# Two-operand steps on VectorE instead of GpSimd, and modulation emitted later, in a two-layer transformer

## The chip, the cores and the metric

One core of a Trainium2 chip. The time is device microseconds of one execution, as the median of several runs; a profiled execution is taken beside them. The engines are TensorE (PE in the profile, with PEld its weight loads), VectorE (DVE), ScalarE (ACT), GpSimd (POOL) and SyncE (SP), whose queue issues all DMAs.

## The reference, cut to what matters

Two layers over 1024 latent tokens and 256 context tokens, 1024 features, all in float32. Each has a mixer (attention) and a feed-forward part with a convolution along the tokens; after each part comes a layer norm of the residual, and both are modulated by vectors computed from a condition.

```python
def conv_ffn(h, w_gate, w_up, conv_w, conv_b, w_down):
    g = h @ w_gate
    gp = jnp.pad(g, ((0, 0), (1, 1), (0, 0)))
    g = gp[:, :-2] * conv_w[0] + gp[:, 1:-1] * conv_w[1] + gp[:, 2:] * conv_w[2] + conv_b
    return (jax.nn.silu(g) * (h @ w_up)) @ w_down

def modulation(cond, w_mod, b_mod):
    return jnp.split(jax.nn.silu(cond) @ w_mod + b_mod, 6, axis=-1)

for i in range(DEPTH):                     # DEPTH = 2
    sh1, sc1, gt1, sh2, sc2, gt2 = modulation(c, w_mod[i], b_mod[i])
    o = mixer(x * (1 + sc1) + sh1)
    x = layer_norm(ALPHA * x + gt1 * o, ln1_g[i], ln1_b[i])
    f = conv_ffn(x * (1 + sc2) + sh2, ...)  # D_FF = 2816 = 22 x 128
    x = layer_norm(ALPHA * x + gt2 * f, ln2_g[i], ln2_b[i])
# the context tokens take the same path in layer 0 with c_ctx
```

## The kernel before

Features lie on partitions and tokens on the free axis. Every float32 product is made of three fp32r matmuls: each operand is split into a high part (ScalarE, `hi`, L82) and a low part (source minus high part, `lo`, L85), and high x high, high x low and low x high are added in PSUM (`mm`, L88). `lo` runs on GpSimd unless an engine is named.

The latent tokens come in two tiles of 512 (t = 0, 1), the context is t = 2. The stages are: layer 0's projections and attentions, `mixer_out` (output product, norms), `conv_ffn(N, 0)`, layer 1's projections and attention, `mixer_end`, `conv_ffn(N, 1)`.

**The feed-forward part** (`FeedForward`) multiplies 2 x 2 blocks with seven products, P1 to P7, instead of eight. In the up half, each of the 22 blocks f of 128 hidden features takes seven steps, one for each P; a step is 12 matmuls of 128x512 (four k, three part products). The tokens' operands of P6, P7, P5, P4 and P3 need both token tiles, those of P1 and P2 only tile 0. So P1 and P2 of the first `EARLY` = 8 blocks are done first (16 steps, here the first phase), while the norm of tile 1 and its operands (`norm`, `norm_operands`, `pair`) are still computed; their results go to DRAM (`pre_d`) and are read back (`again`). Then follow the other five steps of these 8 blocks (early blocks) and all seven of the other 14 (later blocks): 154 steps in all. `prepare` makes a step's weight operand: a sum of weight blocks where the P needs one (`add`, L1254, on VectorE), then its high and low part (`split`). `advance` prepares up to `RING` = 6 steps ahead. `evacuate` adds PSUM results on VectorE (L1364, tiles u, g, v); after P3, `finish` makes the convolution (L1391, L1392, on VectorE), the SiLU (ScalarE) and the product with v (L1394, GpSimd), and stores the block in DRAM (`hid_d`). `down_sums` forms sums of `w_down` blocks for the down half and stores them (`sum_d`), one pair of blocks after each odd f.

In the down half 77 steps follow: for each P, 11 steps j of 12 matmuls into four PSUM banks, with weights from `w_down` or `sum_d` and the hidden blocks read back into SBUF (`leave`, `load_hidden`) as tokens' operands. `hidden_operand` forms sums of hidden blocks (L1254, L1316, L1318) into a tile `sum`; `evacuate` adds each P's banks to the residual (`more`, L1476) at the end of its 11 steps. The hidden blocks of the second half and the residual of tile 1 are loaded when the up half ends.

**Modulation of layer 1** (`mod_vectors`) is computed on VectorE inside layer 0's up half: 12 chunks of 512 columns, each 8 products of a 128x512 tile of `w_mod` with a scalar per partition (L174, L176; for the first four chunks with two conditions, so twice as many), then the sum over partitions by small matmuls with a vector of ones (L183). It is a generator with 4 yields to a chunk; from the first early block on, each step runs it to its next yield.

**The norms** are generators too, in a list `behind`. `tick`, called after every third matmul, runs the first of them to its next yield, so that their work lies between matmuls. `norm` sums the eight feature tiles (partly on GpSimd, L336), takes the mean by a matmul (L359), subtracts it, squares (ScalarE) and sums, takes the statistics by small matmuls (L376), spreads the factor over partitions by a matmul (L273), and scales; k = 2, 5, 7 of the subtractions and scalings are GpSimd's (L346), from a copy of the PSUM tile by ScalarE (L341), the others VectorE's (L348).

`context` computes layer 0's feed-forward part of the context tokens, with 66 weight tiles in a row, each split in two halves.

The order of each engine's instructions is set by a scheduler from the order of emission and from priorities: weight loads are placed ahead by `rush` (100 instructions in the feed-forward parts), the ticks of layer 1's feed-forward part by `chain` (80). The engines then run their instructions in that order. All DMAs are in SyncE's queue, in order.

## Time and profile before

| | us |
|---|---|
| median of 3 runs | 3734.98 (3730.98 to 3742.63) |
| profiled execution, time | 3729.65 |
| profiled execution, span | 3727.8 |
| TensorE busy | 3273.4 |
| VectorE busy | 2668.0 |
| GpSimd busy | 1802.2 |
| ScalarE busy | 1653.1 |

The profile is of one execution; times in it are from the span's start. The profiled execution's own time is 1.85 us more than its span. A row of a group names the line, the engine, the operation, the tiles written and read, their shape and the count, then busy time and the mean of one in ns, then the idle time of the engine just before them and what ended it. A row of a stage gives start and end, length, and for each engine busy time and, in brackets, its instructions; then the granted clock of TensorE (1.00 is full speed), the busy share of the 16 DMA engines and GB/s. A row of a wait gives who waited, for whom, the sum in us, the count and the longest. L88, L82, L85 and L1254 are helpers' lines, so the tile names tell which use is meant: `al<-raw,ah` is the low part of a weight operand, `sum<-affy,siluc,sum` a product of modulation. Line numbers are those of the kernel before.

### The profile page before, as it was taken

Reading aid. Unit: us, or ns where it says so; the run is one execution under the profiler, and the core shown is the slowest. Engines: PE = TensorE matmul, PEld = TensorE weight load, DVE = VectorE, ACT = ScalarE, POOL = GpSimd, SP = SyncE. Lnnn points to the kernel's source line nnn. Section 1 sums busy time; section 2 is a strip of 40 time slices with the busy share of each in tenths; the row PEclk is TensorE's granted clock in tenths of the full one; section 3 lists DMA queues with packets and bytes.
Section 4 is the critical chain, followed back from the end, with each engine's and each line's share of the span. In section 5 each row is a group of like instructions: output and inputs, shape, how many; then the busy total and the mean of one; then the engine's idle time right before and its main releaser. Section 6 shows DMA issues by size and latency. Waiting matters only on the chain. (4 is left out here: it accounts for less than half of the span.)

```text
span 3727.8 us, 49048 instructions
## 1 busy us (share of the span) xinstructions
PE 3273.4 (88%) x16844; PEld 2667.7 (72%) x16844; DVE 2668.0 (72%) x4124; ACT 1653.1 (44%) x3153; POOL 1802.2 (48%) x1316
## 2 busy tenths in 40 slices
PE   8989999997666899898699999999899888999895
PEld 4467788885554688676598887887787666777674
DVE  2148888846777777589698467778897577776695
ACT  3126788824311233343454345556675432333333
POOL 4254344317633466455765334434423666665445
PEclk9999999998777899999799999999999889999997
DMA  7675143134456534633355665557554354345422
GB/s 222 200 209 175 60 102 86 48 108 140 145 168 204 172 128 144 257 91 108 118 178 164 187 179 159 142 157 208 167 153 137 116 173 165 131 144 201 162 84 71
DMA packets 282249, 555.55 MB, mean 149 GB/s; under 512 B 24144, under 2 KB 110608, under 8 KB 279952
## 3 DMA queue, kind: packets, MB, share of 16 engines
q1 hardware_dynamic: 282000, 552.42, 47.2%
q8 instruction: 133, 2.18, 0.2%
q14 instruction: 116, 0.95, 0.1%
HBM read 410.97 MB, written 141.36 MB: 148 GB/s over the span
## 5 line engine op out<-in xcount | busy, mean ns | idle before, releaser
L85 POOL TENSOR_TENSOR al<-raw,ah 128x512 fp32r<-128x512 f32 x374 | 561.8, 1510 | 352.7 <-ACT ah L82 335.9
L82 ACT ACTIVATE ah<-raw 128x512 fp32r<-128x512 f32 x418 | 255.1, 624 | 349.2 <-PE f L88 143.6
L85 POOL TENSOR_TENSOR al<-sum,ah 128x512 fp32r<-128x512 f32 x176 | 261.3, 1500 | 270.7 <-ACT ah L82 265.8
L88 PE MATMUL s<-k,q 128*128 128x512 f32 (+2 forms) x1152 | 306.7, 388 | 14.5 <-ACT sxc L1858 6.6
L85 DVE TENSOR_TENSOR ptl<-tp,pth 128x512 fp32r<-128x512 f32 x412 | 279.6, 684 | 43.3 <-ACT pth L544 38.6
L544 ACT ACTIVATE pth<-tp 128x512 fp32r<-128x512 f32 x412 | 241.8, 594 | 109.8 <-PE tp L540 103.4
L82 ACT ACTIVATE ah<-sum 128x512 fp32r<-128x512 f32 x264 | 161.0, 622 | 290.2 <-PE f L88 201.7
L88 PE MATMUL f<-al,ah 128*128 128x512 f32 x616 | 255.2, 414 | 33.2 <-DVE al L85 33.1
L540 PE MATMUL tp<-ident,p 128*128 128x128 f32 x1648 | 257.4, 276 | 20.4 <-DVE ptl L85 10.2
L88 PE MATMUL f<-ah,ah 128*128 128x512 f32 x616 | 247.9, 410 | 25.1 <-ACT ah L82 24.8
L88 PE MATMUL f<-ah,al 128*128 128x512 f32 x616 | 250.4, 407 | 3.2 <-POOL al L85 3.2
L88 PE MATMUL o<-pth,v 128*128 128x256 f32 x976 | 232.9, 300 | 4.6 <-ACT pth L544 4.5
L540 PEld LDWEIGHTS tp<-ident,p 128*128 128x128 f32 x1648 | 198.0, 142 | 51.6 <-DVE ptl L85 10.1
L88 PEld LDWEIGHTS s<-k,q 128*128 128x128 f32 (+1 forms) x1152 | 189.3, 192 | 44.4 <-ACT p L1871 9.9
L88 PE MATMUL o<-ptl,v 128*128 128x256 f32 x656 | 186.0, 295 | 17.6 <-DVE ptl L85 16.7
L85 POOL TENSOR_TENSOR wl<-wraw,wh 128x1024 fp32r<-128x1024 f32 x36 | 91.1, 2530 | 205.6 <-ACT wh L82 203.7
L88 PEld LDWEIGHTS o<-pth,v 128*128 128x128 f32 x976 | 171.6, 192 | 24.1 <-ACT pth L544 7.9
L1868 DVE TENSOR_REDUCE stat<-s 128x1 f32<-128x1024 f32 x128 | 155.5, 1216 | 37.8 <-PE s L88 37.3
L1871 ACT ACTIVATE p<-s,stat 128x1024 f32<-128x1024 f32 x128 | 142.5, 1114 | 79.9 <-DVE stat L1869 64.7
L1048 POOL TENSOR_SCALAR p<-p,stat 128x1280 f32<-128x1280 f32 (+1 forms) x80 | 94.0, 1178 | 172.3 <-ACT pth L544 59.5
L88 PEld LDWEIGHTS f<-al,ah 128*128 128x128 f32 x616 | 120.8, 196 | 77.4 <-DVE al L85 52.2
L88 PE MATMUL f<-T,ah 128*128 128x512 f32 x528 | 170.1, 404 | 0.2 <-DVE u L1364 0.2
(453 smaller groups left out, 10072.9 us busy)
## 6 DMA issues: line engine op xcount, KB each, us to landing
raw<-w_gate SPq DMA_DIRECT2D x82, 512.0 KB, 3.8
raw<-w_up SPq DMA_DIRECT2D x66, 512.0 KB, 4.7
raw<-w_down SPq DMA_DIRECT2D x66, 512.0 KB, 3.7
wm<-w_mod SPq DMA_DIRECT2D x96, 256.0 KB, 4.2
affy<-w_mod SPq DMA_DIRECT2D x96, 256.0 KB, 3.0
sd<-affy SPq DMA_DIRECT2D x88, 256.0 KB, 5.9
hid<-acc SPq DMA_DIRECT2D x44, 512.0 KB, 2.6
raw<-sd SPq DMA_DIRECT2D x88, 256.0 KB, 2.6
```

The source lines that it names most:

```text
L82: return self.nc.scalar.activation(out, src, AF.Copy)
L85: (eng or self.nc.gpsimd).tensor_tensor(out, src, hi.bitcast(F32), op=ALU.subtract)
L88: self.nc.tensor.matmul(out, lhsT, rhs, start=start, stop=stop)
L540: nc.tensor.transpose(ps[:, n * P : (n + 1) * P], pt[:, kc : kc + P], N.ident[:, :])
L544: nc.scalar.activation(h[:, : n * P], ps[:, : n * P], AF.Copy)
L1048: nc.gpsimd.tensor_scalar(p, p, st[:, 5, b : b + 1], 1.0, op0=ALU.mult, op1=ALU.mult)
L1868: nc.vector.tensor_reduce(st[:, 2, b, m : m + 1], s[:, :], axis=AX.X, op=ALU.max)
L1871: nc.scalar.activation(p[:, :SEQ], s[:, :], AF.Exp, bias=mx, scale=scale, accum_out=sums[:, b, m, 0:1])
```

## The change

- Norms: all sums over feature tiles run on VectorE into one total; of the subtractions k = 2, 5 stay on GpSimd; all scalings run on VectorE from PSUM, without the copy; one pass of statistics matmuls instead of two. `lag` = 3 yields are added in three places ahead of the matmuls. In `norm_parts` and `pair` some affine steps move to ScalarE, and `pair`'s last two low parts to VectorE.
- Modulation: its tiles are loaded two ahead into the tag `opt` (2 buffers, before `affy` with 3); a chunk has 6 yields, one of them between its last product and its matmuls; 72 yields are spread evenly over the 130 steps of the rest of the up half.
- `EARLY` is 12 instead of 8: 24 steps in the first phase (P1 of two blocks, then P2 of both), 12 early and 10 later blocks.
- Low parts of weight operands: on VectorE in the first phase; then GpSimd keeps P2, P7, P4 in the up half, and P5, P6, P4 in the down half. In `context` VectorE takes the first half of each tile.
- `finish`: the product with the gate runs on VectorE and writes s instead of v; the store of block f-1 is issued after P7 of block f. The last block's store, its load and the load of the second residual are issued after the second step of the down half.
- `down_sums` runs after P6 of each f below 11.
- Down half: the order is P1, P2, P5, P6, P7, P4, P3, and the sums of hidden blocks are made in place. The evacuations' VectorE instructions are queued (`late`) and emitted one after each group of three matmuls.

```diff
         nc = self.nc
+        todo = [(k, 1024 * which + 512 * half) for which, half, _ in chunks for k in range(KT)]
+        ws = []
+        def fetch():
+            k, c0 = todo.pop(0)
+            ws.append(self.t(wpool, [P, 512], tag="opt", bufs=2))
+            self.load(ws[-1][:, :], self.ins["w_mod"][l, k * P : (k + 1) * P, c0 : c0 + 512])
+        fetch()
+        fetch()
+        yield
...
             acc = {c: self.t(wpool, [P, 512], tag=f"sum{c}", bufs=1) for c in cs}
-            c0 = 1024 * which + 512 * half
             for k in range(KT):
-                w = self.t(wpool, [P, 512], tag="affy", bufs=3)
-                self.load(w[:, :], self.ins["w_mod"][l, k * P : (k + 1) * P, c0 : c0 + 512])
+                w = ws.pop(0)
...
                         nc.vector.scalar_tensor_tensor(acc[c][:, :], w[:, :], s, acc[c][:, :], op0=ALU.mult, op1=ALU.add)
-                if k % 2 and k < KT - 1:
+                if todo:
+                    fetch()
+                if k % 2:
                     yield
+            yield
...
         x = [self.acc[t][:, k, c0 : c0 + w] for k in range(KT)]
-        gp = (2, 5, 7)
+        gp = (2, 5)
...
-        def total(g):
-            return self.t(tmp, [P, 512], tag=f"{sums}{int(g)}", bufs=1)[:, :w]
-        def add(acc, k, src):
-            g = k in (1, 2, 5)
-            eng = nc.gpsimd if g else nc.vector
-            if g not in acc:
-                acc[g] = src
-                return
-            new = total(g) if any(acc[g] is y for y in x) else acc[g]
-            eng.tensor_tensor(new, acc[g], src, op=ALU.add)
-            acc[g] = new
+        def total(i):
+            return self.t(tmp, [P, 512], tag=f"{sums}{i}", bufs=1)[:, :w]
...
         def each(k, ps, c, op):
-            if k in gp:
+            if c is not None and k in gp:
...
         yield
-        acc = {}
-        for k in range(KT):
-            if k == KT - 1:
-                nc.vector.tensor_tensor(acc[False], acc[False], acc[True], op=ALU.add)
-            add(acc, k, x[k])
+        acc = total(0)
+        for k in range(1, KT):
+            nc.vector.tensor_tensor(acc, x[0] if k == 1 else acc, x[k], op=ALU.add)
...
                 yield
+        for _ in range(self.lag):
+            yield
         mean = psum()
-        nc.tensor.matmul(mean[:, :w], self.mean[:, :], acc[False], start=True, stop=True)
+        nc.tensor.matmul(mean[:, :w], self.mean[:, :], acc, start=True, stop=True)
...
         c = copy(mean)
-        acc, sq = {}, {}
+        acc, sq = total(1), {}
...
             if 1 <= k <= KT:
-                sq[k - 1] = total(k == 2) if k < 3 else self.t(tmp, [P, 512], tag="affy", bufs=3)[:, :w]
+                sq[k - 1] = acc if k == 1 else self.t(tmp, [P, 512], tag="affy", bufs=3)[:, :w]
                 nc.scalar.activation(sq[k - 1], x[k - 1], AF.Square)
-            if k >= 2:
-                add(acc, k - 2, sq[k - 2])
+            if k >= 3:
+                nc.vector.tensor_tensor(acc, acc, sq[k - 2], op=ALU.add)
+            yield
+        for _ in range(self.lag):
...
         for b in range(nb):
-            for g in (True, False):
-                nc.tensor.matmul(st[:, b : b + 1], acc[g][:, b * P : (b + 1) * P], self.mean[:, 0:1],
-                                 start=g, stop=not g)
+            nc.tensor.matmul(st[:, b : b + 1], acc[:, b * P : (b + 1) * P], self.mean[:, 0:1], start=True, stop=True)
...
         r = self.rstd(tmp, st[:, :nb], nb, 1.0, eps)
-        yield
-        yield
+        for _ in range(2 + self.lag):
+            yield
...
         yield
-        c = copy(bc)
...
             if k < KT:
-                each(k, bc, c, ALU.mult)
+                each(k, bc, None, ALU.mult)
...
             self.lo(h[1][:, k, :], ys[k][:, :w], h[0][:, k, :], eng=nc.vector)
-            if keep and k % 2:
+            if keep and k % 4 != 3:
...
             self.hi(t4[0][:, k, :], b)
-            self.lo(t3[1][:, k, :], c, t3[0][:, k, :], pool)
-            self.lo(t4[1][:, k, :], b, t4[0][:, k, :], pool)
+            self.lo(t3[1][:, k, :], c, t3[0][:, k, :], vec)
+            self.lo(t4[1][:, k, :], b, t4[0][:, k, :], vec)
             nc.scalar.activation(xa, xa, AF.Identity, scale=v[:, 2, k : k + 1], bias=v[:, 3, k : k + 1])
-            pool.tensor_scalar(xb, xb, v[:, 2, k + 4 : k + 5], v[:, 3, k + 4 : k + 5], op0=ALU.mult, op1=ALU.add)
+            nc.scalar.activation(xb, xb, AF.Identity, scale=v[:, 2, k + 4 : k + 5], bias=v[:, 3, k + 4 : k + 5])
...
-    ORDER = ("P1", "P2", "P6", "P7", "P5", "P4", "P3")
-    EARLY = 8
+    UP = ("P1", "P2", "P6", "P7", "P5", "P4", "P3")
+    DOWN = ("P1", "P2", "P5", "P6", "P7", "P4", "P3")
+    EARLY = 12
...
         self.raws, self.sums, self.parts = {}, {}, {}
-        first = [(f, p) for f in range(self.EARLY) for p in self.ORDER[:2]]
-        early = [(f, p) for f in range(self.EARLY) for p in self.ORDER[2:]]
-        rest = [(f, p) for f in range(self.EARLY, NF) for p in self.ORDER]
-        down = [(p, j) for p in self.ORDER for j in range(NF // 2)]
+        first = [(f + i, p) for f in range(0, self.EARLY, 2) for p in ("P1", "P2") for i in range(2)]
+        early = [(f, p) for f in range(self.EARLY) for p in self.UP if p not in ("P1", "P2")]
+        rest = [(f, p) for f in range(self.EARLY, NF) for p in self.UP]
+        down = [(p, j) for p in self.DOWN for j in range(NF // 2)]
...
             p, j = self.steps[n]
-            a = self.split(self.raws.pop(n))
+            a = self.split(self.raws.pop(n), None if p in ("P5", "P6", "P4") else self.N.nc.vector)
...
             src = self.add(a12, s[2], ALU.subtract)
-        self.parts[n] = self.split(src)
+        self.parts[n] = self.split(src, None if p in ("P2", "P7", "P4") and n >= self.n_first else self.N.nc.vector)
...
             return self.add(b12, b11, ALU.subtract)
-        t = self.add(b22, b12, ALU.subtract)
+        put = self.N.nc.vector.tensor_tensor
+        if p == "P6":
+            put(b12, b22, b12, op=ALU.subtract)
+            put(b11, b12, b11, op=ALU.add)
+            return b11
         if p == "P7":
-            return t
-        nc = self.N.nc
-        nc.vector.tensor_tensor(t, t, b11, op=ALU.add)
-        if p == "P4":
-            nc.vector.tensor_tensor(t, b21, t, op=ALU.subtract)
-        return t
+            return b12
+        put(b21, b21, b11, op=ALU.subtract)
+        return b21
...
             nc.scalar.activation(s, s, AF.Silu)
-            nc.gpsimd.tensor_tensor(v, v, s, op=ALU.mult)
-            N.load(self.hid_d[f][:, :], v)
-        ready = None
+            nc.vector.tensor_tensor(s, v, s, op=ALU.mult)
+        def store(f):
+            N.load(self.hid_d[f][:, :], s)
+        span, gone = self.n_up - self.n_first, 0
...
             if n >= self.n_first:
-                next(mods, None)
-                if p == "P6" and f % 2:
-                    self.down_sums(f // 2)
-                if p == "P4" and f + 1 < self.EARLY:
-                    ready = f + 1
+                while gone < 72 * (n - self.n_first) // span:
+                    next(mods, None)
+                    gone += 1
+                if p == "P6" and f < NF // 2:
+                    self.down_sums(f)
+                if p == "P7" and f:
+                    store(f - 1)
                 if p == "P3":
-                    if ready == f + 1:
-                        again(ready)
+                    if f + 1 < self.EARLY:
+                        again(f + 1)
+                    if f == NF - 1:
+                        self.leave(p)
                     finish(f)
-            if f == NF - 1:
+            if f == NF - 1 and p != "P3":
                 self.leave(p)
+        self.last = lambda: (store(NF - 1), self.load_hidden(1, (NF // 2 - 1,)), self.load_residual(1))
...
             self.places += [N.t(N.pbig, [P, 4, SEQ], tag=x) for x in ("b1h", "b1l")]
-            self.load_hidden(1, range(4, h))
-            self.load_residual(1)
+            self.load_hidden(1, range(4, h - 1))
...
+        late = collections.deque()
...
             a = N.acc[t][:, m, :]
-            nc.vector.scalar_tensor_tensor(a, src, gt[:, m : m + 1], a, op0=ALU.mult, op1=ALU.add)
+            late.append(lambda: nc.vector.scalar_tensor_tensor(a, src, gt[:, m : m + 1], a, op0=ALU.mult, op1=ALU.add))
...
                 more(0, 0, d, y)
-            elif p == "P6":
-                nc.vector.tensor_tensor(y, ps, y, op=ALU.add)
-                more(1, 0, d, y)
-            elif p == "P7":
-                nc.vector.tensor_tensor(y, ps, y, op=ALU.add)
-                more(0, 1, d, y)
-                more(1, 1, d, y)
...
                 more(1, 0, d, ps)
+            elif p == "P6":
+                late.append(lambda: nc.vector.tensor_tensor(y, ps, y, op=ALU.add))
+                more(1, 0, d, y)
+            elif p == "P7":
+                late.append(lambda: nc.vector.tensor_tensor(y, ps, y, op=ALU.add))
+                more(0, 1, d, y)
+                more(1, 1, d, y)
...
-        last = NF // 2 - 1
+        final = NF // 2 - 1
...
             if j == 0:
-                banks = [N.t(N.qq, [P, 512], tag="f") for _ in range(4)]
+                bank = [N.t(N.qq, [P, 512], tag="f") for _ in range(4)]
...
                 c = slice(d * P, (d + 1) * P)
-                ps = banks[d][:, :]
+                ps = bank[d][:, :]
...
                 N.mm(ps, ah[:, c], bl[:, :], False, False)
-                N.mm(ps, al[:, c], bh[:, :], False, j == last)
+                N.mm(ps, al[:, c], bh[:, :], False, j == final)
+                if late:
+                    late.popleft()()
                 N.tick()
-                if j == last:
+                if j == final:
                     evacuate(p, d, ps)
-            if j == last and p in ("P4", "P3"):
+            if n == self.n_up + 1:
+                self.last()
+            if j == final and p in ("P4", "P3"):
+                while late:
+                    late.popleft()()
...
                 r = raws[i]
-                parts.append([self.split(r[:, 512 * x : 512 * x + 512], nc.vector if x and i % 3 else None) for x in range(2)])
+                parts.append([self.split(r[:, 512 * x : 512 * x + 512], None if x else nc.vector) for x in range(2)])
```

2 lines of the change are left out of this document (added).

## The prediction

> **What bounds the kernel now.** I read the page first (busy shares and the slices), then busy time by stage, then the waits and groups of the worst stage, then single rows. TensorE is busy for 88% of the span, but three slices in a row show a granted clock of 0.7:
>
> ```profile
> PE 3273.4 (88%) x16844; PEld 2667.7 (72%) x16844; DVE 2668.0 (72%) x4124; ACT 1653.1 (44%) x3153; POOL 1802.2 (48%) x1316
> ...
> PEclk9999999998777899999799999999999889999997
> ```
>
> The stages that the change touches, in the order of the rows below: layer 0's first phase, its early blocks, a steady stretch inside the later blocks, all later blocks, the turn from up to down, down, down's last phase; then layer 1's first phase, up, turn, down, last phase, and the tail.
>
> ```profile
> core 0: us, PE busy (x) PEld busy (x) DVE busy (x) ACT busy (x) POOL busy (x), PEclk, DMA share, GB/s
> 911.00:985.50 74.50, 56.17 (x212) 43.12 (x212) 45.32 (x52) 34.02 (x59) 60.51 (x43) 0.82 0.50 172
> 985.50:1245.60 260.10, 155.01 (x593) 125.04 (x593) 201.97 (x268) 49.65 (x66) 93.89 (x56) 0.75 0.59 187
> 1300.00:1500.00 200.00, 200.00 (x862) 162.36 (x861) 148.49 (x152) 69.79 (x104) 129.81 (x82) 1.00 0.39 130
> 1245.60:1523.30 277.70, 277.06 (x1193) 224.85 (x1194) 210.85 (x226) 91.76 (x135) 170.52 (x107) 0.99 0.42 138
> 1523.30:1577.00 53.70, 37.01 (x133) 26.84 (x132) 24.94 (x23) 16.74 (x28) 19.28 (x12) 0.87 0.94 360
> 1577.00:1744.00 167.00, 155.63 (x662) 124.00 (x662) 149.32 (x165) 64.21 (x112) 82.81 (x56) 0.99 0.34 104
> 1744.00:1801.70 57.70, 45.69 (x155) 33.60 (x154) 38.15 (x43) 26.65 (x45) 45.29 (x34) 0.79 0.23 66
> 2929.80:3013.00 83.20, 58.95 (x221) 45.10 (x221) 57.61 (x61) 37.19 (x65) 68.68 (x49) 0.82 0.47 149
> 3013.00:3419.20 406.20, 389.92 (x1647) 310.33 (x1648) 303.89 (x314) 130.43 (x195) 256.87 (x157) 0.99 0.44 145
> 3419.20:3471.80 52.60, 37.31 (x134) 26.25 (x133) 23.18 (x25) 16.60 (x28) 16.52 (x11) 0.90 1.00 385
> 3471.80:3646.00 174.20, 162.24 (x677) 129.02 (x678) 156.88 (x172) 66.86 (x116) 88.46 (x61) 0.97 0.29 87
> 3646.00:3689.10 43.10, 35.98 (x136) 27.01 (x134) 25.64 (x30) 16.43 (x29) 27.14 (x21) 0.88 0.22 76
> 3689.10:3727.80 38.70, 7.85 (x20) 4.57 (x20) 17.02 (x23) 8.72 (x14) 17.25 (x15) 0.55 0.15 54
> ```
>
> 862 matmuls in 200 us are 0.232 us each, so a step (12 matmuls) is 2.78 us. Layer 0's 40 early steps are worth 111 us and took 260.1. Layer 1, which has no modulation to compute, took 406.2 us for 138 steps worth 384. What held layer 0's early steps:
>
> ```profile
> PE f L183 <- DVE sum L176: 99.7, 9, 18.4
> DVE modv L187 <- PE f L183: 15.8, 9, 2.8
> DVE sum L1254 <- DMA raw<-w_up: 11.6, 3, 6.0
> SPq L75 <- DVE sum L176: 65.1, 59, 4.0
> ...
> 1131.90 1.86 PE L183 MATMUL f<-ones,sum 128*128 128x1 f32 x8 [11.21 <-DVE sum L176]
> ```
>
> TensorE stands before modulation's column sums (L183) until VectorE has run through the products (L176), nine times, up to 18.4 us: one yield in each step puts modulation's 48 yields into 48 steps. VectorE is the near-bound there (202 of 260 us), and GpSimd makes it slower:
>
> ```profile
> L1364 DVE TENSOR_TENSOR acc<-f,acc 128x512 f32<-128x512 f32 x72 | 48.0, 683 | 22.4 <-DMA hid<-acc 20.0 <-DVE acc L1364 1.0 <-PE f L88 0.5
> L1392 DVE SCALAR_TENSOR_TENSOR acc<-acc,vecs 128x1023 f32<-128x1023 f32 x10 | 22.0, 2198 | 0.4
> L1254 DVE TENSOR_TENSOR sum<-raw,sum 128x512 f32<-128x512 f32 x10 | 15.8, 1577 | 3.9 <-POOL al L85 3.9
> L1391 DVE SCALAR_TENSOR_TENSOR acc<-acc,vecs 128x1023 f32<-128x1023 f32 x10 | 12.8, 1285 | 13.7 <-ACT acc L1390 13.7
> L1254 DVE TENSOR_TENSOR affy<-affy,raw 128x512 f32<-128x512 f32 x5 | 12.3, 2463 | 0.0
> L1254 DVE TENSOR_TENSOR sum<-raw,raw 128x512 f32<-128x512 f32 x10 | 6.8, 678 | 0.0
> L85 POOL TENSOR_TENSOR al<-raw,ah 128x512 fp32r<-128x512 f32 x31 | 45.8, 1491 | 6.7 <-ACT ah L82 6.7
> ```
>
> (The steady stretch.) The same two-operand form takes 0.678 us or up to 2.463; with one operand in PSUM (L1364) it is always 0.683. Over the three slow groups shown, the excess is 15.8-6.8, 12.3-3.4 and 22.0-12.8, 27 us; with the smaller groups about 40 us for 82 GpSimd instructions: an estimate of 0.5 us of VectorE for each.
>
> Single costs, uncontended:
>
> ```profile
> 3714.77 3.08 DVE L348 TENSOR_TENSOR acc<-acc,f 128x512 f32<-128x512 f32 x5 [2.86 <-ACT bcs L341]
> 3714.81 3.72 POOL L346 TENSOR_TENSOR acc<-acc,bcs 128x512 f32<-128x512 f32 x3 [3.63 <-ACT bcs L341]
> 3718.51 3.02 POOL L1610 TENSOR_SCALAR acc<-acc,vecs 128x512 f32<-128x512 f32 x4
> 1010.05 2.72 DVE L176 SCALAR_TENSOR_TENSOR sum<-affy,siluc,sum 128x512 f32<-128x512 f32 x4
> L85 DVE TENSOR_TENSOR wl<-wraw,wh 128x1024 fp32r<-128x1024 f32 x44 | 55.8, 1269 | 27.9 <-ACT wh L82 27.4
> ```
>
> In a row, VectorE does a 512-wide two-operand step each 3.08/5 = 0.62 us (GpSimd 1.24), a product 0.68, a 1024-wide step 1.27.
>
> **The change, part by part.**
>
> *Up, layer 0 (the largest term).* After the first phase 130 steps remain (12 blocks of 5, 10 of 7), 361 us of TensorE and some 17 us of column sums (an estimate: 16 groups, each 1.86 us at most by the row above, which ran at a low clock, so near 1 us). VectorE now has, in the 12 early blocks: evacuations 72, weight sums 48, down-sums 44 (now one block each, f<11), low parts 36 (P6, P5, P3): 200 x 0.62 = 124 us. Each block's end is two 1023-wide steps and the product that was GpSimd's, 2 x 1.28 + 1.27 = 3.8, x12 = 46. Modulation's 72 yields now lie over 130 steps, 33 of them here, with some 76 products: 52 us. Together 222 us against 167 of TensorE: VectorE becomes the bound of this stretch, and the covers it gave for nothing are gone. To it come 24 GpSimd low parts x 0.5 = 12, and waits. The waits (weights landing, modv: 27.4 us by the rows above) I bound by zero and by twice those rows, 55; I take about 25, since as many turns of the four weight buffers wait as before. In them lies SP's queue: modulation's loads now go through two buffers instead of three, each waits there for the product that frees one, as it did before (65.1 us), and pre's loads, hid's and the sums' stores stand behind; the weight loads are issued ahead of it. Early: 259 us. The 10 later blocks: VectorE 150 x 0.62 + 38 + 35 + 15 = 181, under TensorE's 195 + 7 = 202. Together 461. Before, the same 130 steps cost 537.8 (260.1 + 277.7) less 8 steps, 22.2, which now belong to the first phase: 515.6. **-54 us.**
>
> *Up, layer 1.* The same without products: early 124 + 46 + 12 + about 17 of waits = 199 against TensorE's 167; later 195. 394 against 406.2 - 22.2 = 384: **+10 us.** Here the change costs: the down-sums crowd into the 12 short blocks. What it gives back: hid's store no longer holds v (20.0 us of VectorE's idle in the steady stretch, hidden there by six prepared steps), so it counts nothing.
>
> *First phase.* 24 steps, 66.7 us, and 8 of norm matmuls. VectorE: norm 29, operand pairs 40, low parts 24, evacuations 12: 105 x 0.62 = 65, and 11 GpSimd steps x 0.5 = 6. In before the pairs pass between GpSimd and VectorE and TensorE runs dry after 16 steps; now it has 8 more. I take 82 (75 and 7 of stalls) in layer 0, 87 in layer 1, against 74.5 + 22.2 and 83.2 + 22.2: **-15, -18.** The longer norms (39 yields for 30, by the lag) no longer fit the 64 ticks of the pass before, so some of norm 2 is drained in front of the first phase: **+3** (between 0 and 8).
>
> *The turn from up to down.* It moves 360 and 385 GB/s with a DMA share of 0.94 and 1.00, so bytes are time here.
>
> ```profile
> raw<-w_down SPq DMA_DIRECT2D x66, 512.0 KB, 3.7
> sd<-affy SPq DMA_DIRECT2D x88, 256.0 KB, 5.9
> acc<-res SPq DMA_DIRECT2D x4, 2048.0 KB, 12.8
> ```
>
> The last down-sums (2 x 512 + 4 x 256 KB) are now eleven blocks earlier, and residual 1 (2048 KB) and the last hid load are issued two steps into down: 4.2 MB / 0.385 = 11 us, and SP's queue no longer holds weight loads behind the last store. I take **-10 each**; none if the hid loads alone fill the queues.
>
> *Down.* 662 and 677 matmuls (55 and 56 steps) are worth 154 and 157 us and took 167 and 174.2.
>
> ```profile
> PE f L88 <- DVE al L85: 15.2, 20, 2.2
> ```
>
> (Layer 1's down.) Sums in place cut P6, P7, P4 from 2, 1, 3 instructions to 2, 0, 1; with both low parts VectorE has at most 3 steps, 1.9 us, in a step of 2.78, and evacuations are spread one per slice. **-13 each.** In the last phase VectorE has 55 steps, 34 us (norm, 22 low parts, late sums), against 39 of TensorE: layer 0 from 57.7 to 44, **-13**; layer 1, **-5**.
>
> *Rest.* Tail: one matmul pass fewer and no ACT copy before the scaling, GpSimd's 3.72 off the end, against 3 more VectorE sums of 0.62: **-4**. The last mixer's norms **-3**. Context: a low part moves to VectorE in each triple (+), the norm at its start stalls less (-): 0. ACT's extra affine steps lie under its 56% of idle.
>
> Sum: 3 - 15 - 18 - 54 + 10 - 20 - 26 - 18 - 3 - 4 = -145. The profiled execution ran 3729.65 us (span 3727.8), so 3584.7; the median of the runs is 5.3 above it: **3590 us**.
>
> *A rule against the change.* Five steps in 3.08 us overlap their ends; alone one is 0.683. The Trainium skill ("VectorE: DVE Perf Modes", The DRAIN you can't avoid) says that the next operation does not start until the pipe is empty. By that rule the sum would be 3627 (the last of the rivals); by the row of five in 3.08 us it is 3590, and the rule does not hold here.
>
> **The rivals.**
>
> *VectorE keeps pace* (contention and waits vanish): early stretches 222 and 170 instead of 259 and 199: 3590 - 66 = 3524. For it: L1364's steady 0.683. Against: 24 low parts stay on GpSimd in each.
>
> *The stall stays* (the change doesn't do what it says): VectorE, in order, runs so late that TensorE still meets the column sums too early; layer 0's up stays at 515: 3644. For it: 222 us of VectorE in 167 us of steps. Against: sums are emitted two yields, about 3.6 steps, after their products.
>
> *VectorE binds both layers, and it gets slower.* If a two-operand step keeps costing what contention makes of it, up and the first phases run at VectorE's pace. With a cost r times 0.62, the early stretches grow by 392(r - 1) less the 24 counted for contention, layer 0's later blocks (166r) pass their 202 at r = 1.22, and each first phase (65r) its 85 at 1.31. At r = 1.36 (0.84 us a step) that is 117 + 24 + 7 = 148 and the gain is gone; at 1.45 it is 152 + 39 + 18 = 209, or 3799. For it: the steady stretch's sums cost 0.68 to 2.46. Against: GpSimd, 129.81 of 200 us there, falls to 24 steps in 259 us.
>
> *Operations do not overlap their ends*: the 610 two-operand steps of both early stretches (2 x 200) and first phases (2 x 105) at the single row's 0.683 instead of 0.62: 3590 + 37 = 3627. The five in 3.08 us speak against it.
>
> **How the numbers follow.** Forecast 0.62 (its own range 3545 to 3635), VectorE keeps pace 0.12, the stall stays 0.13, ends don't overlap 0.02, VectorE binds 0.11, of which a third ends within 0.3% of before, which is about what a measurement of this kernel can tell from no change. Faster 0.89, same 0.04, slower 0.07. The range goes from 3505 (VectorE keeps pace, turn and down at their best) to 3690 (the stall stays, and the wait bound of 55).
>
> **What would show it.** Right: no wait of L183 over 3 us; layer 0's up near 461 us, VectorE over 90% busy in its early blocks and its L1254 near 0.7 us; layer 1's early blocks slower than 2.78 us a step; no 13 us hole after the first phase; turns under 45 us. Wrong: L1254 still over 0.84 us, or TensorE still waiting for L176 by tens of us, or weight loads late behind SP's in-order waits.

## The result and the profile after

The changed kernel takes 3519.35 us in the median (3515.21 to 3524.63, four runs), the kernel before on the same chip 3738.81 (3730.98 to 3752.69): a ratio of **0.941, 95% interval 0.9378 to 0.9442**. The forecast was 3590. Its profiled execution took 3515.21 us (span 3513.4), against 3729.65 before: -214 where -145 was forecast. The line numbers have moved: high parts L82 are now L84, low parts L85 are L87, matmuls L88 are L90, products L176 are L187, column sums L183 are L197, weight sums L1254 are L1257, evacuations L1364 are L1369, and a block's end L1391, L1392, L1394 is L1396, L1397, L1399.

The page's busy times and granted clock:

```profile
PE 3205.5 (91%) x16772; PEld 2632.9 (75%) x16772; DVE 2650.5 (75%) x4518; ACT 1674.3 (48%) x3161; POOL 1097.7 (31%) x848
...
PEclk9999999999888899999899999999999999999998
```

GpSimd lost 705 us of work and VectorE has none the more in total, although it took most of these steps over. The stages, in order: layer 0's first phase, early blocks, later blocks, the hole at the turn (in which TensorE has next to nothing to do), the first part of down; the last mixer; layer 1's first phase, early blocks, later blocks, turn; and the tail.

```profile
core 0: us, PE busy (x) PEld busy (x) DVE busy (x) ACT busy (x) POOL busy (x), PEclk, DMA share, GB/s
904.80:992.60 87.80, 77.51 (x301) 60.38 (x302) 71.00 (x108) 47.32 (x82) 19.25 (x13) 0.88 0.61 203
992.60:1234.70 242.10, 198.69 (x793) 160.49 (x792) 226.75 (x325) 61.16 (x83) 37.94 (x24) 0.85 0.75 246
1234.70:1435.30 200.60, 200.60 (x889) 163.42 (x887) 174.66 (x253) 71.41 (x101) 36.67 (x28) 1.00 0.50 158
1435.30:1452.90 17.60, 1.81 (x9) 1.71 (x9) 7.16 (x8) 2.90 (x3) 0.00 (x0) 0.65 1.04 403
1452.90:1489.00 36.10, 36.10 (x150) 29.68 (x151) 20.94 (x34) 15.91 (x28) 0.00 (x0) 0.93 0.74 260
...
2728.00:2790.70 62.70, 56.86 (x232) 44.58 (x232) 44.70 (x63) 24.39 (x33) 19.37 (x14) 0.95 0.44 147
2790.70:2869.30 78.60, 72.36 (x301) 56.76 (x302) 70.74 (x107) 47.48 (x81) 19.48 (x13) 0.98 0.56 187
2869.30:3053.00 183.70, 174.05 (x721) 137.88 (x720) 172.17 (x223) 58.75 (x80) 46.33 (x23) 0.97 0.79 264
3053.00:3249.00 196.00, 196.00 (x841) 157.68 (x840) 146.08 (x193) 72.49 (x104) 40.03 (x29) 1.00 0.29 98
3249.00:3285.00 36.00, 32.72 (x135) 26.00 (x134) 22.39 (x33) 15.96 (x27) 0.00 (x0) 0.95 0.98 374
...
3480.20:3513.40 33.20, 6.00 (x13) 2.78 (x12) 19.60 (x32) 8.64 (x13) 6.61 (x7) 0.58 0.17 63
```

Both later stretches of up are full (TensorE 200.60 of 200.60 and 196 of 196). What is left lies in layer 0's early blocks (VectorE busy for 94%, TensorE 43 us short), the hole behind up, and the tail. Against the forecast's terms, with 22.2 us for the eight steps that moved into each first phase:

| part | forecast | measured |
|---|---|---|
| up to the first phase / context and odd attention / last mixer / tail | +3, 0, -3, -4 | -6.2, -14.2, -9.7, -5.5 |
| first phases, layers 0 and 1 | -15, -18 | -8.9, -26.9 |
| up after them, layers 0 and 1 | -54, +10 | -72.9, -4.2 |
| turn and down, layers 0 and 1 | -36, -28 | -27.2, -38.6 |
| sum | -145 | -214.3 |

The miss of 69 us is in two rows: 32 in the first (norms), 33 in the third (up). The second and the fourth row are near the forecast only as sums: in each, one layer gained 6 to 9 us less than forecast and the other 9 to 11 more. And the second and third row of layer 1 hang on a bound: the forecast ended the first phase of the kernel before at 3013.0, behind a hole; the table of stages below ends it at the next stage's first matmul, 2994.3. By that bound 18.7 us move from the one row to the other (-8.2 and -22.9 for -26.9 and -4.2).

What TensorE waited for most in layer 0's early blocks (the waits), and groups of VectorE there:

```profile
PE f L197 <- DVE sum L187: 39.1, 5, 12.2
```

```profile
L187 DVE SCALAR_TENSOR_TENSOR sum<-opt,siluc,sum 128x512 f32<-128x512 f32 x66 | 50.8, 812 | 2.3 <-DMA opt<-w_mod 2.2
...
L87 DVE TENSOR_TENSOR al<-sum,ah 128x512 fp32r<-128x512 f32 x35 | 28.7, 821 | 0.1
...
L1257 DVE TENSOR_TENSOR affy<-raw,affy 128x512 f32<-128x512 f32 x11 | 12.5, 1138 | 0.0
...
L1257 DVE TENSOR_TENSOR sum<-raw,sum 128x512 f32<-128x512 f32 x12 | 8.1, 678 | 0.0
```

The column-sum wait fell from 99.7 us to 39.1 but is there still. VectorE has next to no idle time, so the wait is no latency that a few yields could hide: VectorE is late because it is full. The same form costs 0.678 us or 1.138, as GpSimd works beside it or not; single rows of both are in the last section.

The hole at the turn, in order of time (timeline of VectorE, ScalarE and TensorE):

```profile
1443.40 1.24 ACT L1395 ACTIVATE acc<-acc,vecs 128x1024 f32<-128x1024 f32 x1 [7.51 <-DMA hid<-acc]
1444.68 1.28 DVE L1396 SCALAR_TENSOR_TENSOR acc<-acc,vecs 128x1023 f32<-128x1023 f32 x1 [7.28 <-ACT acc L1395]
...
1449.61 1.53 DVE L187 SCALAR_TENSOR_TENSOR sum<-opt,siluc,sum 128x512 f32<-128x512 f32 x2
...
1451.20 1.87 PE L197 MATMUL f<-ones,sum 128*128 128x1 f32 x8 [15.79 <-DVE sum L187]
```

The last products of modulation stand in VectorE's queue behind the last block's end, which stands behind the store of the block before. Spread over all 130 steps, modulation ends where nothing is left to hide it.

### The profile page after: what moved, and what is told of

Same layout as the page of the kernel before. It is cut to its first block, busy times and chain, and to the rows that moved or that the text cites. A ratio compares the mean times of both kernels' runs of the same rounds, so it can differ in the third digit from the quotient of the medians.

```text
span 3513.4 us, 48532 instructions
## 1 busy us (share of the span) xinstructions
PE 3205.5 (91%) x16772; PEld 2632.9 (75%) x16772; DVE 2650.5 (75%) x4518; ACT 1674.3 (48%) x3161; POOL 1097.7 (31%) x848
## 5 line engine op out<-in xcount | busy, mean ns | idle before, releaser
L87 POOL TENSOR_TENSOR al<-raw,ah 128x512 fp32r<-128x512 f32 x196 | 296.9, 1516 | 665.6 <-ACT ah L84 652.2
L84 ACT ACTIVATE ah<-raw 128x512 fp32r<-128x512 f32 x418 | 260.5, 630 | 434.3 <-PE f L90 294.8
L90 PE MATMUL s<-k,q 128*128 128x512 f32 (+2 forms) x1152 | 307.7, 389 | 15.8 <-ACT sxc L1877 6.8
L87 DVE TENSOR_TENSOR ptl<-tp,pth 128x512 fp32r<-128x512 f32 x412 | 279.6, 684 | 42.2 <-ACT pth L546 37.2
L84 ACT ACTIVATE ah<-sum 128x512 fp32r<-128x512 f32 x198 | 122.0, 629 | 342.9 <-DVE sum L1257 172.6
L542 PE MATMUL tp<-ident,p 128*128 128x128 f32 x1648 | 257.6, 276 | 20.7 <-DVE ptl L87 10.2
L90 PE MATMUL f<-al,ah 128*128 128x512 f32 x616 | 245.5, 398 | 10.5 <-DVE al L87 10.3
L90 PE MATMUL f<-ah,al 128*128 128x512 f32 x616 | 243.3, 395 | 7.5 <-POOL al L87 7.5
L90 PE MATMUL f<-ah,ah 128*128 128x512 f32 x616 | 241.3, 395 | 3.0 <-ACT ah L84 3.0
L90 PE MATMUL o<-pth,v 128*128 128x256 f32 x976 | 232.7, 300 | 4.6 <-ACT pth L546 4.5
L87 DVE TENSOR_TENSOR al<-raw,ah 128x512 fp32r<-128x512 f32 x222 | 173.7, 795 | 77.9 <-ACT ah L84 77.8
L90 PEld LDWEIGHTS s<-k,q 128*128 128x128 f32 (+1 forms) x1152 | 189.9, 193 | 45.7 <-ACT p L1890 10.8
L87 POOL TENSOR_TENSOR al<-sum,ah 128x512 fp32r<-128x512 f32 x44 | 67.8, 1541 | 426.0 <-ACT ah L84 384.3
L90 PE MATMUL o<-ptl,v 128*128 128x256 f32 x656 | 185.8, 295 | 16.3 <-DVE ptl L87 15.6
L90 PEld LDWEIGHTS o<-pth,v 128*128 128x128 f32 x976 | 171.2, 192 | 24.2 <-ACT pth L546 7.9
L1890 ACT ACTIVATE p<-s,stat 128x1024 f32<-128x1024 f32 x128 | 142.7, 1115 | 82.9 <-DVE stat L1888 67.6
L90 PE MATMUL f<-T,ah 128*128 128x512 f32 x528 | 168.7, 401 | 1.2 <-ACT ah L84 1.2
L90 PE MATMUL f<-b0h,ah 128*128 128x512 f32 x352 | 143.8, 409 | 14.4 <-ACT ah L84 8.8
L87 POOL TENSOR_TENSOR wl<-wraw,wh 128x1024 fp32r<-128x1024 f32 x36 | 91.2, 2533 | 202.7 <-ACT wh L84 200.8
```

The costliest lines, as they stand in the source:

```text
L84: return self.nc.scalar.activation(out, src, AF.Copy)
L87: (eng or self.nc.gpsimd).tensor_tensor(out, src, hi.bitcast(F32), op=ALU.subtract)
L90: self.nc.tensor.matmul(out, lhsT, rhs, start=start, stop=stop)
L542: nc.tensor.transpose(ps[:, n * P : (n + 1) * P], pt[:, kc : kc + P], N.ident[:, :])
L1890: nc.scalar.activation(p[:, :SEQ], s[:, :], AF.Exp, bias=mx, scale=scale, accum_out=sums[:, b, m, 0:1])
```

## The experiments

All are edits of the changed kernel; ratios are to the kernel before. Stage times of their profiles in us: the bounds are the first matmuls that read the next stage's operands; the hole at the turn is within "later 0"; kernels with 8 early blocks have 16 steps in the first phase and 40 in the early blocks, for 24 and 60.

| kernel | start | first 0 | early 0 | later 0 | down 0 | odd | mixer | first 1 | early 1 | later 1 | down 1 | tail | span |
|---|---|---|---|---|---|---|---|---|---|---|---|---|---|
| before (8 early) | 911.0 | 74.5 | 260.1 | 277.7 | 278.2 | 1052.9 | 75.4 | 64.5 | 139.0 | 285.9 | 269.8 | 38.7 | 3727.8 |
| changed | 904.8 | 87.8 | 242.1 | 218.2 | 233.4 | 1038.7 | 65.7 | 78.5 | 183.8 | 196.0 | 231.2 | 33.2 | 3513.4 |
| norms back | 914.6 | 90.3 | 237.1 | 218.1 | 241.6 | 1045.2 | 73.5 | 86.9 | 185.0 | 195.2 | 235.2 | 38.2 | 3561.0 |
| GpSimd back | 901.3 | 84.6 | 272.4 | 235.5 | 232.7 | 1039.8 | 66.4 | 78.8 | 203.6 | 200.2 | 231.8 | 33.2 | 3580.3 |
| eager modulation | 899.6 | 89.8 | 292.4 | 204.8 | 234.5 | 1042.0 | 65.5 | 78.5 | 184.8 | 196.0 | 233.3 | 33.2 | 3554.4 |
| pacing 22 + 50 | 903.0 | 86.7 | 210.6 | 226.0 | 234.1 | 1038.2 | 65.5 | 78.3 | 184.6 | 195.2 | 234.6 | 33.2 | 3490.0 |
| modulation on TensorE | 904.7 | 86.6 | 211.1 | 241.7 | 234.1 | 1041.9 | 65.9 | 78.2 | 188.7 | 195.2 | 231.7 | 33.2 | 3513.0 |
| turn back | 902.6 | 89.6 | 242.0 | 218.5 | 233.4 | 1042.7 | 67.1 | 79.9 | 184.9 | 195.2 | 230.4 | 33.2 | 3519.4 |
| down back | 903.5 | 89.8 | 242.9 | 218.3 | 244.9 | 1043.5 | 65.5 | 78.6 | 184.0 | 196.0 | 245.2 | 33.2 | 3545.3 |
| 8 early blocks | 903.3 | 64.8 | 163.1 | 308.1 | 232.8 | 1041.8 | 67.6 | 60.4 | 124.8 | 275.1 | 229.9 | 33.2 | 3505.0 |
| sums back | 903.2 | 86.6 | 220.0 | 235.2 | 233.2 | 1035.2 | 65.6 | 78.5 | 168.8 | 201.6 | 236.2 | 33.6 | 3497.6 |
| no GpSimd | 903.1 | 86.7 | 240.4 | 218.0 | 233.2 | 1042.0 | 65.5 | 78.6 | 185.1 | 195.2 | 233.6 | 33.6 | 3514.9 |
| split modulation | 904.7 | 88.1 | 199.3 | 206.1 | 233.9 | 1043.8 | 66.9 | 78.6 | 186.7 | 195.2 | 232.9 | 33.3 | 3469.5 |
| sums spread too | 900.0 | 89.8 | 198.9 | 219.9 | 234.2 | 1044.1 | 65.8 | 78.4 | 172.8 | 195.8 | 230.2 | 33.9 | 3463.7 |

Where an edit does not touch them, start lies between 899.6 and 904.8, odd between 1035 and 1044, and each of the other stages within 5 us.

**Norms back.** `norm`, `norm_parts` and `pair` as in the kernel before; a line of `pair`:

```
-            self.lo(t3[1][:, k, :], c, t3[0][:, k, :], vec)
+            self.lo(t3[1][:, k, :], c, t3[0][:, k, :], pool)
```

> The changed kernel (3515.21 us profiled), with the token norms and the last mixer's VectorE steps as in the kernel before: steps and sums shared with GpSimd, two chains of sums, a copy of the scaling factor, no extra yields ahead of TensorE's sums. Theory of the forecast: outside the first phases the norms are worth little (start +3, context 0, last mixer -3, tail -4, last phases some -5), so the time comes back by 9 us, and by some 6 in each first phase through GpSimd's contention: about 3535. Rival, from the changed kernel's stages (start -6, context -9.5, last mixer -9.7, tail -5.5, all without an edit other than the norms' in front of them): the norms alone hold 31 us there and 10 to 20 in the first phases: 3555 to 3570, with TensorE again 8 us late for the first sum at the context's start.

3563.49 us, ratio 0.9561 (0.9545 to 0.9578): the rival is right. The norms hold 48 us: start 9.8, odd 6.5 (no more than it varies by), mixer 7.8, tail 5.0, together 29; layer 1's first phase 8.4; the downs, with their last phases, 8.2 and 4.0. TensorE again waits 7.6 us for the first sum at the context's start. Where the time goes is seen in TensorE's waits in the last mixer, first with the norms back, then in the changed kernel:

```profile
PE f L90 <- ACT wh L84: 6.1, 1, 6.1
PE f L390 <- POOL sum L350: 3.0, 1, 3.0
PE f L90 <- DVE wl L87: 2.1, 1, 2.1
```

```profile
PE f L380 <- DVE sum L373: 4.6, 1, 4.6
PE f L90 <- ACT wh L84: 0.5, 1, 0.5
```

The wait for the norm's own sum is no shorter (4.6 for 3.0). What went is the wait for the next weights, 8.2 us, whose two parts stand behind the norm's steps in ScalarE's and VectorE's queues: with the norms back, the ScalarE step in front of `wh` itself waits 1.8 us for GpSimd.

**GpSimd back.** `self.parts[n] = self.split(src)` in up, and the block's last product on GpSimd.

> The changed kernel with all low parts of up's weight operands and each block's last product on GpSimd again; modulation, norms, down and the 12 early blocks stay changed. Theory A (VectorE's time bounds the early blocks, and each GpSimd instruction costs it 0.5 to 0.8 us): in layer 0's early blocks VectorE loses 36 low parts and 12 products (38 us) and gains 48 GpSimd instructions (24 to 38 us), so they stay within 15 us of 242; the first phases lose VectorE 24 low parts each. In all 3490 to 3530. Theory B (the move to VectorE carries up's gain): the early blocks of both layers and the first phases come back towards the time before, 3560 to 3600, with VectorE's sums at over 1.2 us and low parts late.

3584.40, ratio 0.962 (0.9602 to 0.9637): theory B's time, and its early blocks: layer 0's lose 30 us, layer 1's 20. Its first phases did not come: they are no longer than the changed kernel's (84.6 and 78.8 for 87.8 and 78.5). Window and groups of layer 0's early blocks, then what TensorE waited for there and in layer 1's:

```profile
985.90:1258.30 272.40, 198.43 (x794) 160.21 (x793) 238.16 (x288) 64.63 (x91) 128.67 (x75) 0.82 0.69 224
```

```profile
L187 DVE SCALAR_TENSOR_TENSOR sum<-opt,siluc,sum 128x512 f32<-128x512 f32 x64 | 68.6, 1115 | 0.7 <-DMA opt<-w_mod 0.7
...
L1257 DVE TENSOR_TENSOR sum<-raw,sum 128x512 f32<-128x512 f32 x13 | 13.1, 1011 | 1.9 <-POOL al L87 1.9
```

```profile
PE f L197 <- DVE sum L187: 69.6, 5, 20.9
```

```profile
PE f L90 <- POOL al L87: 19.9, 19, 2.4
```

In layer 0 VectorE does 37 instructions fewer (288 for 325) and is busy 11 us longer: a product costs 1.115 us for 0.812. Taking off the 36 low parts at 0.68 and 11 products of a block's end at 1.22 leaves 189 of 226.75; it was busy 238, 49 us more, of which some 5 are other steps that fell into the window: some 45 us for 51 more GpSimd instructions. In layer 1 (busy 168.82 for 172.17) the same sum gives 29 us for 48, where 36 were saved. **A step handed to GpSimd costs VectorE about as much as doing it.** The time goes two ways: in layer 0 the products come later, and the column sums' wait grows from 39.1 us to 69.6; in layer 1, which has no products, TensorE waits 19.9 us for GpSimd's own low parts (4.1 in the changed kernel).

**Eager modulation** (`next(mods, None)` once a step) and **pacing 22 + 50**:

```
-                while gone < 72 * (n - self.n_first) // span:
+                i, e = n - self.n_first, 5 * self.EARLY
+                while gone < (22 * i // e if i < e else 22 + 50 * (i - e) // 62):
```

> The changed kernel with one yield of modulation in each step again, so that its 72 lie in the first 72 of 130 steps. Theory A (VectorE's time is the bound in layer 0's early blocks): 27 more yields, some 42 products at 0.68 to 0.77 us, fall into them, and they grow from 242 by about 30; the later blocks stay at TensorE's pace, and the 15.8 us wait of the column sum at the turn goes: about 3530. Theory B (TensorE's waits there are the latency of each group of sums, not VectorE's load): the early blocks stay within 8 us of 242 plus the sums that moved in (5 groups of 1.9 us), and the turn gains 16: about 3505.

> The changed kernel with 22 of modulation's 72 yields in the 60 early steps (33 before) and the other 50 in the 62 steps after, none in the last 8. Theory A (VectorE bounds the early blocks, with 15 us of idle; the later blocks have 26 us of VectorE to spare): early 242 - 11 x 112/72 x 0.77 = 229, later unchanged at 200 to 203, the turn without its 15.8 us wait: about 3487. Theory B (waits are latency): early stays at 235 to 242, later grows by the sums, the turn still gains: about 3500. Theory C (the later blocks have no room left): later over 210, about 3500 with VectorE at over 95% there.

3556.24 (0.9545, 0.9527 to 0.9563) and 3493.44 (0.9375, 0.9358 to 0.9391). In the early blocks theory A in both, and more than it said: they go from 242 to 292 (30 more expected) and to 210.6 (229 expected). Early blocks of the eager one, its waits, and the paced one, with a wait of its later blocks:

```profile
989.30:1281.70 292.40, 209.72 (x825) 170.17 (x824) 251.65 (x375) 63.05 (x83) 35.84 (x24) 0.80 0.71 236
```

```profile
PE f L197 <- DVE sum L187: 82.7, 9, 14.4
DVE acc L1369 <- PE f L90: 20.8, 13, 3.6
```

```profile
989.60:1200.20 210.60, 188.01 (x769) 146.55 (x768) 200.46 (x281) 57.77 (x79) 38.74 (x23) 0.94 0.76 256
```

```profile
PE f L197 <- DVE sum L187: 13.8, 4, 10.2
```

A product costs more than its own 0.77 us. At a column sum TensorE, in order, stands still though operands are ready (ScalarE waits 87.4 us there for TensorE to free their buffers, for 36.3 in the changed kernel); then VectorE has no evacuations to do and idles in its turn (20.8 us for 2.8), so the two take turns. With fewer products TensorE meets the sums late enough, the wait for L187 falls to 0.9 us, and VectorE alone sets the pace (200.46 of 210.60). The later blocks took the rest (218.2 with the hole, 226.0 without): TensorE meets column sums too early there now, once by 10.2 us, so part of the gain is given back. This is theory C's sign (over 210), though VectorE is busy for 92% there, not 95%.

**Modulation on TensorE.** Products and column sums replaced by

```
+                    nc.tensor.matmul(ps[:, 128 * j : 128 * j + m], w[:, j * P : (j + 1) * P], self.siluc[:, k, :m],
+                                     start=k == 0 and j == 0, stop=k == KT - 1 and j == 3)
```

> The changed kernel with modulation's products left to TensorE: for each 128-row piece of the weights four matmuls with a 128x1 or 128x2 silu operand add up in one PSUM bank (384 small matmuls in place of 112 VectorE products and 16 groups of column sums); loads and pacing stay, through four buffers. Theory A (VectorE's time is what holds layer 0's up): 112 x 0.77 = 86 us leave VectorE, TensorE pays 384 x 0.12 = 46 less 15; layer 0's early blocks come to 190 to 200 (layer 1 takes 183.8 without products), all of its up, turn wait included, to 415 to 430 from 460.3: about 3475. Theory B (waiting at the modulation is latency of its loads, whoever computes): TensorE now waits for the weights' DMA instead and the early blocks stay above 225: 3500 or more.

3510.69 (0.9414, 0.94 to 0.9428), no faster than the changed kernel. The time is theory B's (3500 or more), but not by its cause: the early blocks come to 211, not over 225, and TensorE waits for the weights' DMA 3.2 us in all of up. Early and later blocks:

```profile
991.40:1202.50 211.10, 207.94 (x1058) 175.20 (x1057) 177.45 (x248) 61.37 (x83) 34.73 (x24) 0.98 0.82 275
1202.50:1444.10 241.60, 241.60 (x1257) 204.67 (x1256) 143.55 (x204) 72.62 (x101) 36.08 (x28) 1.00 0.43 141
```

VectorE is freed as theory A has it, but my price for TensorE was wrong. Its busy time in up is 449.5 for 361 of steps, so the 384 matmuls cost some 88 us, 0.23 each; each is recorded as two, and I had taken the record's 0.12 for the matmul.

**Turn back, down back.**

```
-        self.last = lambda: (store(NF - 1), self.load_hidden(1, (NF // 2 - 1,)), self.load_residual(1))
+        store(NF - 1); self.load_hidden(1, (NF // 2 - 1,)); self.load_residual(1)
```

and for the other `hidden_operand`, `run_down`, the order of the phases and the low parts' engine as before.

> The changed kernel with the last store of the hidden blocks, the last hidden load and the second residual's load issued at the end of up again, not two steps into down. Theory of the forecast (bytes bound the turn; each turn gained about 10 us through these later issues and the earlier sums together): down with its turn grows by some 5 us in each layer from 233.4 (layer 0) and 231.2 (layer 1), 3525. Rival (the hidden loads alone fill the queues; the turn's gain comes from the down-sums' earlier place): no stage moves by more than 2 us, 3515.

> The changed kernel with down's inner part as before: token sums in new tiles (2, 1 and 3 instructions for P6, P7, P4), weight operands' low parts all on GpSimd, evacuations at once after each phase, the order of the phases as in up; the late loads stay. Theory of the forecast: -13 in each layer's down and part of the last phase's -13 and -5 come back: down from 233.4 and 231.2 to about 250 each, 3548. Rival (down's gain came from the turn and from the norms in its last phase): under 5 us in each layer, 3520.

3521.22 and 3547.09 (one run each). The late issues are worth nothing (233.4 and 230.4 in the downs): the rival. Down's inner part is worth 11.5 and 14.0, with what it does in the last phase: near the forecast's 13 each, and under the 17 and 19 that were expected here with a part of the last phases' terms.

**8 early blocks** (`EARLY = 8`).

> The changed kernel with 8 early blocks in place of 12. Theory A (up is bound by VectorE, which has about 18 us of work a block in layer 0, against 13.9 us of TensorE's in an early block and 19.5 in a later one): four blocks that become later ones are no longer held, layer 0's first phase and up go from 548 to about 533, layer 1's from 458 to 450: about 3492. Theory B (the eight steps more of the first phase are what the norms of the second half are hidden behind): the first phases run dry again by 15 to 20 us each before the first P6, and the time is 3515 to 3545.

3509.22 (0.9412, 0.9396 to 0.9428). First phase and up come to 536.0 in layer 0 (548.1 with 12) and 460.3 in layer 1 (458.3). So 12 blocks cost layer 0 some 12 us, as theory A has it, and nothing in layer 1, where it expected 8 us. Theory B holds in kind: with 8 blocks TensorE waits 11.2 us (layer 0) and 5.6 us (layer 1) for operands at the end of the first phase, where the changed kernel waits for none. In layer 1 the two about cancel; the medians do not differ enough to tell the two kernels apart.

**Sums back** (`if p == "P6" and f % 2: self.down_sums(f // 2)`) and **no GpSimd** (all of up's low parts on VectorE).

> The changed kernel with the weight sums for down made in every second block again, the last two sets in blocks 19 and 21 just ahead of the turn; all else stays. Theory A (the turn's gain, which the later loads did not make, came from the sums' place: their 2 x 512 + 4 x 256 KB a block no longer meet the hidden loads): layer 1's turn loses 10 to 15 us again (down with its turn from 231.2 to 241 or more); at the same time the early blocks lose half of the sums (24 VectorE steps, 15 us): layer 1's early from 183.8 to about 172, layer 0's from 242 to about 225. In all 3495 to 3515. Theory B (the turn's gain is the shorter VectorE queue of down's first steps): down stays within 3 us of 231 to 234, and only the early blocks gain: 3485.

> The changed kernel with the last low parts of up's weights (P7, P4 and the later P2: 24 in each early stretch, 30 in each later one) on VectorE too, so that GpSimd does nothing there. It prices one GpSimd instruction on VectorE's time. Each low part costs VectorE 0.68 us of its own; if a GpSimd instruction slows VectorE by 0.5 us (the forecast's estimate), VectorE's busy time in layer 1's early blocks rises from 172 by about 4 us, if by 1.0 (which the kernel with the low parts back on GpSimd gave for layer 0), it falls by about 8; layer 0's early blocks from 226.8 likewise. In all 3505 at 1.0, 3525 at 0.5, and later blocks unchanged, since VectorE has room there.

3499.38 and 3516.66 (one run each). Sums in every second block give the early blocks 22 and 15 us, more than theory A expected. Layer 1's later blocks lose 5.6, and its down 5.0, no more than downs vary by, where theory A expected 10 to 15; layer 0's down loses nothing (233.2), and its later blocks with the hole lose 17, the column sum at the turn now waiting 24.5 us. The time is theory A's (3495 to 3515); that the sums' place makes the turn's gain is not shown. Without GpSimd, layer 0's and layer 1's early blocks:

```profile
989.70:1230.20 240.50, 200.85 (x794) 160.18 (x793) 221.42 (x345) 60.79 (x84) 0.00 (x0) 0.87 0.74 243
...
2867.50:3052.50 185.00, 174.21 (x721) 134.17 (x720) 167.84 (x246) 58.09 (x79) 0.00 (x0) 0.99 0.77 260
```

VectorE's busy time falls though it does 20 and 23 steps more: own work +13.6 and +15.6 (0.68 each), the sum -5.3 and -4.3, so the 24 and 23 GpSimd steps had cost it 19 and 20 us: 0.8 and 0.87 each, not 0.5. (In a row a step adds only 0.60; by that it is 0.7 and 0.8.) And the forms are back at one price: the 1.138 us of a weight sum in layer 0 are 0.682, layer 1's L1397 takes 1.278 for 1.936. The time stays all the same, between the two that were expected: in layer 1 VectorE waits for the weights instead, 12.8 us for 7.5:

```profile
DVE sum L1257 <- DMA raw<-w_up: 12.8, 10, 3.6
```

**Split modulation.** The four groups with two columns on TensorE as above, the other eight on VectorE, 24 yields in the early steps and 48 in the next 62. **Sums spread too:** the same with 30 + 42 yields and

```
+    SUMS = (0, 2, 4, 6, 8, 10, 12, 13, 14, 15, 16)
-                if p == "P6" and f < NF // 2:
+                if p == "P6" and f in self.SUMS:
```

> The changed kernel with modulation's first four groups (two columns each, 64 VectorE products) added up by TensorE (32 pieces x 4 matmuls, which the trace records as two each of 0.12 us: 30 us), the other eight groups (64 products) on VectorE as before, and 24 of the 72 yields in the early steps, 48 in the 62 after. Theory (up ends when the busier of the two engines does): TensorE 361 + 30 + 8 = 399, VectorE about 177 + 143 + 50 = 370 and its waits; layer 0's up with the turn from 460.3 to 400 to 415, about 3460 in all, against 3490 with the pacing alone. Rival (VectorE, with contention and waits, still sets the pace in the later blocks): later over 215, 3475 or more.

> The kernel with modulation split between TensorE and VectorE, with the weight sums for down in blocks 0, 2, 4, 6, 8, 10, 12, 13, 14, 15 and 16 (six sets in the early blocks, five after, the last five blocks ahead of the turn) and 30 of modulation's yields in the early steps. Theory A (layer 1's early blocks are held by the sums' VectorE steps and bytes; the later blocks have room for five sets; the turn needs the sums out of its way): layer 1's early from 186.7 to about 171, its later and down within 3 us; layer 0's early stays at 197 to 200, where TensorE is full, its later at 203 to 208: about 3440 in all, in a profile some 15 less than the 3469.5 of the split. Rival (layer 0's later blocks, with 193 of 206 us of VectorE, have no room for 14 us of sums): they grow by 8 or more, and the two cancel: 3450 to 3460.

The split gives **3456.98 us, ratio 0.9265 (0.9248 to 0.9283)**, the best here and clear of the changed kernel's 0.9378 to 0.9442. (Its profiled execution, 3471.51, is the slowest of its four.) Its early and later blocks:

```profile
992.80:1192.10 199.30, 196.78 (x962) 163.20 (x961) 174.85 (x237) 60.42 (x81) 35.40 (x23) 0.99 0.81 279
1192.10:1398.20 206.10, 204.68 (x922) 167.07 (x921) 192.66 (x281) 71.94 (x102) 43.67 (x29) 1.00 0.54 179
```

TensorE is busy for 401.46 of 405.4 us, and the stretch is within the 400 to 415 of the theory. Spreading the sums gives 3467.75 (0.929, 0.9269 to 0.9311), not faster: layer 1's early blocks gain 13.9 and layer 0's later ones lose 13.8, as the rival had it.

## Why the prediction was right, and where its sizes were off

The direction was right, and so was where VectorE would bind. The size was not: the change gained half as much again as forecast, and 3519 lies outside the 3545 to 3635 that the forecast gave its own mechanism.

*Right.* VectorE binds layer 0's early blocks (94% busy), the later blocks run at TensorE's pace (200.6 for 202 forecast), weight sums are back at 0.68 us where no GpSimd step is beside them, and the hole of 13 us before the first P6 is gone, in layer 1 too. Down's inner part (-13; undoing it gives back 11.5 and 14.0, the last phase among it) and the tail (-4, measured -5.5) came out near their size.

*Norms (32 us too small).* "Some of norm 2 is drained in front of the first phase: +3" and "Context: 0" failed: these stages gained 6.2 and 14.2, and undoing the norms alone gives back 29 us outside first phases and downs (of the 14.2 only 6.5, in a stage that varies by 9). I had priced the waits for the norm's sums and not what is queued behind its steps: in the last mixer the first did not shrink, and the wait that went is for the next weights' two parts.

*Up (33 us too small).* Layer 0's early blocks: 234 us of VectorE and 25 of waits were forecast; 226.75 and 15.4 were measured, so more than half of the miss is the wait term, carried over from the rows of the kernel before. Layer 1's: 182 and 17, measured 172.2 and 11.5. VectorE does 223 steps in that stretch where the forecast counts 236 (200, and three to each of 12 blocks' ends): two of the last block's three, for one, lie past the bound. At 0.77 us a step, which is 182/236 and 172.17/223 alike, these 13 are the 10 us. So up, which was to lose 10 us here, gained 4. TensorE waits 1.5 us in the first 36 steps, and then, from 2969 to 3053, 8 us for all three engines (GpSimd 4.1, VectorE 2.7, ScalarE 1.2).

The contention price of 0.5 us was too low (0.7 to 0.9 by the run without GpSimd, 0.6 and 0.9 by the one with more of it) and hid in the same sums: with 24 steps left it is 5 to 9 us a layer, and VectorE's own work was sized too high by more than that. It is not all that these steps are worth. With them on GpSimd 67 us come back, and the rows of that run show the loss as later column sums in layer 0 and as late low parts in layer 1: a wait of TensorE for GpSimd itself, which the forecast's terms for up do not have.

*Wrong step.* "No wait of L183 over 3 us" contradicted the forecast's own bound: where VectorE is the bound and TensorE is in order, the lateness must show at some matmul, and it shows at the column sum, up to 12.2 us, and once more at the turn (15.8), which the forecast of -10 for layer 0's turn did not see: its turn, hole included, takes 53.7 us, not under 45. So the forecast's own sign of being wrong, TensorE still waiting for the products by tens of us, is there too (39.1 and 15.8 us, for 99.7): the rival in which the stall stays is in part what happened. Pacing by load, not by steps, takes the first to 0.9 us and removes the second, but brings 13.8 us to the later blocks; with the products split between TensorE and VectorE, TensorE waits for column sums 1.4 us in all.

*The turn.* The rows of layer 1's turn (the waits) in the kernel before, the changed one, and the one with the sums back:

```profile
ACT ah L82 <- DMA raw<-w_down: 18.5, 5, 7.2
...
PE f L88 <- ACT ah L82: 11.9, 4, 4.0
```

```profile
ACT ah L84 <- DMA raw<-w_down: 9.3, 2, 7.2
PE f L90 <- ACT ah L84: 3.0, 1, 3.0
```

```profile
ACT ah L84 <- DMA raw<-w_down: 14.9, 3, 7.3
...
PE f L90 <- ACT ah L84: 5.7, 2, 4.5
```

TensorE waited for operands whose weights came late. The forecast divided the bytes of two causes by 385 GB/s. One of them, the late loads, is worth nothing, as the run with the turn back shows; nor are the queues emptier in the changed kernel's turn (374 GB/s, a DMA share of 0.98), in which TensorE waits only 3.0 us. The other, the sums' place, is worth 3 us in these rows, and at most 5 in layer 1's down. Down's inner part makes 14 of layer 1's -38.6 and the norms 4; what makes the other 15 or more no run here tells apart.

*The rivals.* "VectorE keeps pace" gave 3524, 5 us from the result, and is not what happened: its early stretches of 222 and 170 measured 242 and 184, with VectorE full. The time alone would have picked the wrong story. (In "operations do not overlap their ends", 610 steps at 0.063 us are 38 us, not 37.)

## What to carry to other kernels

Before moving a step between two engines that contend, take the price from both groups: the same form beside the other engine and alone, times the count. Work spread evenly over steps of uneven load makes the loaded ones late: pace it by the room that the windows show, and end it before the stage does. And when an engine is the bound, do not forecast that nobody waits for it: say which in-order instruction will.
